# The bonus in a tile of its own, and the load of r, k, v on ACT's queue

## The chip, the cores and the metric

The kernel runs on one core of one Trainium2 chip. The metric is the device time of one execution in microseconds. The runs of the kernel before took 1875.28, 1884.89 and 1886.19 us, a median of 1884.89 us.

## The reference, cut to what matters

Two layers act on 1024 latent tokens and 256 context tokens of width 1024, all in fp32. The first layer mixes a short convolution with a gated recurrence of 8 heads of 64 (RWKV-7), run once forward and once in reverse. The second layer is latent attention. The change lies in the first layer, where the operands of the recurrence are prepared. For each direction the reference computes

```
decay, k_dir, b_vec = rwkv_direction(k, wl, al, kk, w0[d], w2[d], a0[d], a2[d], k_a)
y, state = rwkv7_scan(r, decay, k_dir, v, -kk, b_vec, state, reverse)
bonus[s] = bonus[s] + jnp.sum(r * k_dir * r_k, axis=-1, keepdims=True) * v
```

and later adds the bonus to the normalised output of the scan. The bonus of a token and a head is one number (the sum of r * k_dir * r_k over the 64 channels of the head, both directions together) times the vector v.

## The kernel before, in words

The input projections of layer 1 (`project`, L431 to L452) are matmuls in three split parts, 24 for each group of 512 tokens, written into two PSUM banks in turn (tag "p"). `shifted` (L536) makes r, k and v of a pair of heads j from them and stores them, with the normalised k, into `rkv_d[j]` in HBM, a tensor of 128 partitions by 4 parts by 1280 tokens (part 0 the normalised k, 1 r, 2 k, 3 v). Other projections (`zb`, `conv`) and the modulation of the layers (`ada`, L153) have no part in the recurrence's operands.

The operand stage (L849 to L883) runs over 20 units: 4 pairs of heads j times 5 groups q of 256 tokens. A unit has four parts. `decays(d)` (L633) makes the decay factors of direction d with two small products on PE, activations on ACT and a running sum on DVE (L647). `operands(d)` (L657) multiplies them with the parts of the unit's tile `x` on DVE: L667 and L668 write the tile AR, L669 and L670 the tile bk, L673 to L676 the tile BK, and in the second direction L680 and L681 write r * k_dir * r_k into x's part 2. `chunks(d)` (L683) forms products of 64-token chunks on PE (L690, L697), masks and copies them (L693 on DVE, L698 on ACT) and writes AR and M to HBM by nine DMAs (L701 to L709). `bonus` (L711) sums part 2 over the channels with a product on PE (L714), multiplies it with v into part 3 of the same tile x on DVE (L715), and writes that part to `bon_d` by two DMAs (L717).

`load_x` (L611) fetches the tile x of a unit, 512 KB, from `rkv_d`. x has two buffers. In the program's text the load for unit n+1 stands ahead of `operands(0)` of unit n (L867), so it takes the buffer that unit n-1 used, and may start when the last reader of that buffer is done.

Between the parts of a unit, `step` (L834) advances the chain of projections and the inversions (`invert`, L731) at the rates of L601. In this stage the order on PE is that of the text (`manual_schedule`, L507); on ACT, DVE, POOL and SP a planner puts the instructions in an order, and each engine and each of its DMA queues then runs its list in that order. ACT's queue issues the weights of the projections (L253) and of the modulation (L159), SP's nearly all other DMAs, POOL's those of the inversions of j below 3. ACT also empties the PSUM banks of the projections (L147 splits the next weights, L457, L467 and L543 read the products), and copies the modulation's product (L172), which PE transposes next (L176) and DVE adds up (L178). Squares of k are summed over the channels on PE at L575 and read on DVE at L576.

Of the kernel before, what the change touches and what calls it, by code (L numbers as in the profile page):

```python
# [9 lines left out]
F32 = mybir.dt.float32  # L10
# [3 lines left out]
ALU = mybir.AluOpType  # L14
# [4 lines left out]
P = 128  # L19
# [32 lines left out]
def build(ctx, tc, I, out, dbg=None):  # L52
    nc = tc.nc
    V, S, G, TE, SY = nc.vector, nc.scalar, nc.gpsimd, nc.tensor, nc.sync
# [12 lines left out]
    rkv_d = [dram.tile([P, 4, T], F32, name=f"rkv_d{j}") for j in range(4)]  # L67
    mix_d = [dram.tile([P, 4, T], F32, name=f"mix_d{i}") for i in range(2)]

    zb_d, bon_d = (dram.tile([P, 4, T], F32, name=n) for n in ("zb_d", "bon_d"))  # L70
# [200 lines left out]
    hs = (slice(0, 64), slice(64, 128))  # L271
# [41 lines left out]
    with ExitStack() as c2:  # L313
# [3 lines left out]
        xs = []  # L317
        for n0 in range(0, T, 256):
            x = x2.tile([P, KT, 256], F32, tag="x", name="x", bufs=5)
# [57 lines left out]
        for i in range(4):  # L377
            rest = []
            for n, x in enumerate(xs):
                s, cols = 1 if n == 0 else 0, slice(n * 256, n * 256 + 256)  # L380
                h, lo = H[:, 2 * i:2 * i + 2, cols], L[:, 2 * i:2 * i + 2, cols]
# [123 lines left out]
    with ExitStack() as c1:  # L505
# [4 lines left out]
        bp = cb.enter_context(tc.tile_pool(name="prep", bufs=1, side="right"))  # L510
        scanm = cc("scan")
        NB, N = 4, 256
# [96 lines left out]
        xs = []  # L609

        def load_x(j, q):  # L611
            xs.append(bp.tile([P, 4, N], F32, tag="x", name="x", bufs=2))
            SY.dma_start(out=xs[-1], in_=rkv_d[j][:, :, q * N:q * N + N])

        def load_w2(j):
            w = lp.tile([P, 2, P], F32, tag="w2", name="w2")
# [11 lines left out]
        def unit(j, q):  # L628

            n0, c0 = q * N, q * NB  # L630
# [80 lines left out]
            def bonus():  # L711
                x = xs.pop(0)
                ps = psb.tile([P, 512], F32, tag="b", name="b")
                TE.matmul(ps[:, :N], bones, x[:, 2], start=True, stop=True)  # L714
                V.tensor_tensor(x[:, 3], x[:, 3], ps[:, :N], op=ALU.mult)  # L715
                for h in range(2):
                    SY.dma_start(out=bon_d[hs[j % 2], j // 2 * 2 + h, n0:n0 + N], in_=x[hs[h], 3])  # L717

            return decays, operands, chunks, bonus

# [131 lines left out]
        split_w2()  # L852
        need(0)
        load_x(0, 0)
        us[0][0](0)
        us[0][0](1)
        for n, (j, q) in enumerate(uo):
            decays, operands, chunks, bonus = us[n]
            after = us[n + 1]
            if q == 4:  # L860
                need(j + 1)
            if q == 2 and j < 3:
                load_w2(j + 1)
            if q == 4 and j < 3:
                split_w2()
            if after:
                load_x(*uo[n + 1])  # L867
            operands(0)
            step(RATE[j][0])
            operands(1)  # L870
            if after:
                after[0](0)
            step(RATE[j][1])
            chunks(0)
            if after:
                after[0](1)
            step(RATE[j][2])
            chunks(1)
            bonus()
            step(RATE[j][3])  # L880
            if q == 4:
                advance(inv, 99)
                inv = invert(j)  # L883
# [71 lines left out]
    with ExitStack() as c1:  # L955
        c1.enter_context(tc.manual_schedule(engines={ET.PE, ET.DVE, ET.Activation}))
        op = c1.enter_context(tc.tile_pool(name="rw_scan0", bufs=1, side="right", reuse_waits="tile"))
# [155 lines left out]
    def products1(wh, wl, n0, n1, pool=ops, tag="o"):  # L1113
        ps = pool.tile([P, 512], F32, tag=tag, name="p")
        gemm3(ps[:, :n1 - n0], lambda kt: wh[:, kt, :], lambda kt: wl[:, kt, :],
              lambda kt: H[:, kt, n0:n1], lambda kt: L[:, kt, n0:n1], KT)
        return ps

    OUTM = {ET.PE}
    with ExitStack() as c1:  # L1120
# [44 lines left out]
        for x, q in enumerate(quarters):  # L1165
            n0, n1 = q * 256, q * 256 + 256
# [3 lines left out]
            xs = []  # L1170
            ps = [ops.tile([P, 512], F32, tag="o", name="o").rearrange("p (a b) -> p a b", a=2) for _ in range(4)]
# [60 lines left out]
    with ExitStack() as c1:  # L1232
# [106 lines left out]
        for x, (m, (n0, n1)) in enumerate(units):  # L1339
# [10 lines left out]
            if (m, n0) in early:  # L1350
                ps = early.pop((m, n0))
            else:
# [3 lines left out]
                ps = products1(*ready[m], n0, n1)  # L1356
# [12 lines left out]
    with ExitStack() as c1:  # L1369
# [196 lines left out]
        for x, (h, n) in enumerate(groups):  # L1566
# [4 lines left out]
            if (h, n) == (7, 0):  # L1571
                cw.close()
                clat.close()
                op = co.enter_context(tc.tile_pool(name="o_p", bufs=2, side="left"))
# [29 lines left out]
    with ExitStack() as c1:  # L1604
# [3 lines left out]
        for m, n0 in [(m + i, n) for m in range(0, 8, 2) for n in (0, 512) for i in range(2)]:  # L1608
# [5 lines left out]
            ps = ops.tile([P, 512], F32, tag="o", name="o")  # L1614
# [107 lines left out]
```

## Time and profile before

| | us |
|---|---|
| median of 3 runs | 1884.89 |
| profiled execution, its own time | 1887.55 |
| span of the profiled execution | 1885.8 |
| PE busy | 1719.4 (91%) |
| DVE busy | 1197.7 (64%) |
| ACT busy | 922.9 (49%) |
| POOL busy | 199.4 (11%) |

PE is TensorE (PEld its weight loads), DVE VectorE, ACT ScalarE, POOL GpSimd, SP SyncE. The operand stage lies between about 115 and 690 us of the span. Busy time is an average over stages; a gap on PE in one stage is read from PE's instructions there and from what ended the gap.

### The profile page before, as it was taken

The page shows a single profiled execution, that of the slowest core. Times are in us where ns is not written, and L with a number is a line of the kernel's source. Part 1 is how long each engine was busy: PE and PEld are TensorE (multiplying, and loading weights), DVE is VectorE, ACT ScalarE, POOL GpSimd, SP SyncE. Part 2 cuts the span into 40 slices and gives each one's busy share as a digit, 9 for nine tenths or more (in the row PEclk, how much of TensorE's full clock was granted, in tenths as well). Part 3 has the DMA queues.
Part 4 walks back from the last instruction along what each step waited for, and adds up shares of the span by engine and source line. Part 5 has one row for each costly group of instructions (what it writes and reads, how often), then busy time and mean ns, then how long its engine had stood idle before and what let it go on. Part 6 is the DMA issues. An engine that isn't in the chain of part 4 may idle for free.

```text
span 1885.8 us, 37021 instructions
## 1 busy us (share of the span) xinstructions
PE 1719.4 (91%) x14352; PEld 1480.7 (79%) x14352; DVE 1197.7 (64%) x2685; ACT 922.9 (49%) x2353; POOL 199.4 (11%) x230
## 2 busy tenths in 40 slices
PE   4999989889999979787899999999998999999999
PEld 3777867767778767776889978788888888888787
DVE  5747559738849745444378662558777777787822
ACT  4756444554444412555244342366666666666610
POOL 1200010220230300010043100000010010010000
PEclk9999999998999989898999999999999999999999
DMA  9067877997996854999644331210000010001242
GB/s 333 26 190 209 229 182 192 254 228 181 229 236 171 217 112 124 345 335 307 228 153 131 108 106 62 85 47 12 21 25 26 20 31 20 21 20 32 93 146 100
DMA packets 264575, 263.31 MB, mean 140 GB/s; under 512 B 63504, under 2 KB 226192, under 8 KB 263056
## 3 DMA queue, kind: packets, MB, share of 16 engines
q1 hardware_dynamic: 220528, 211.82, 38.5%
q10 hardware_dynamic: 37744, 33.03, 6.0%
q0 software_dynamic: 6128, 16.10, 3.7%
q8 instruction: 113, 1.85, 0.4%
q14 instruction: 62, 0.51, 0.1%
HBM read 164.90 MB, written 95.94 MB: 138 GB/s over the span
## 4 chain that ended last, share of the span: by engine, by line
PE 37%; DVE 12%; ACT 6%; DMA 6%; issue 4%; SPq 1%; POOL 0%; ACTq 0%; POOLq 0%; DVEq 0%
PE p L268 8%; PE s_ps L1486 5%; PE o L268 5%; PE p L444 3%; PE po L1525 3%; PE o L1179 3%; PE pk L268 3%; DVE mx L1489 2%; DVE pL L148 2%; PE pT L1513 2%; ACT jk L1436 1%; PE r_ps L1486 1%; DMA X<-v_d 1%; ACT p L1498 1%; PE y L1027 1%
## 5 line engine op out<-in xcount | busy, mean ns | idle before, releaser
L444 PE MATMUL p<-h0H,wh 128*128 128x512 f32 x744 | 277.4, 373 | 8.2 <-DVE th L458 7.3
L444 PE MATMUL p<-h0H,wl 128*128 128x512 f32 x744 | 267.4, 359 | 0.5 <-DVE wl L148 0.5
L444 PE MATMUL p<-h0L,wh 128*128 128x512 f32 x744 | 267.6, 360 | 0.0
L444 PEld LDWEIGHTS p<-h0H,wh 128*128 128x128 f32 x744 | 141.9, 191 | 32.7 <-DVE th L458 7.7
L444 PEld LDWEIGHTS p<-h0H,wl 128*128 128x128 f32 x744 | 141.4, 190 | 23.4 <-DVE wl L148 1.0
L444 PEld LDWEIGHTS p<-h0L,wh 128*128 128x128 f32 x744 | 141.7, 191 | 19.8
L147 ACT CAST pH<-pT 128x512 fp32r<-128x512 f32 x160 | 94.2, 589 | 75.6 <-PE pT L1513 72.9
L148 DVE TENSOR_TENSOR pL<-pT,pH 128x512 fp32r<-128x512 f32 x160 | 109.5, 685 | 30.6 <-ACT pH L147 29.3
L1486 PE MATMUL s_ps<-kH,q 128*128 128x512 f32 x256 | 108.1, 422 | 0.0
L1513 PE MATMUL pT<-cst,p 128*128 128x128 f32 x640 | 98.1, 275 | 10.1 <-DVE mx L1495 3.5
L1489 DVE TENSOR_REDUCE mx<-s_ps 128x1 f32<-128x512 f32 x128 | 87.5, 684 | 22.4 <-PE s_ps L1486 21.9
L1525 PE MATMUL po<-pL,vH 128*128 128x256 f32 x320 | 92.9, 290 | 6.0 <-DVE pL L148 5.2
L1525 PE MATMUL po<-pH,vH 128*128 128x256 f32 x320 | 95.8, 299 | 0.1
L1179 PE MATMUL o<-mh,woH 128*128 128x256 f32 x320 | 93.8, 293 | 0.8 <-DVE y L1074 0.5
L1513 PEld LDWEIGHTS pT<-cst,p 128*128 128x128 f32 x640 | 74.0, 140 | 23.2 <-DVE pL L148 6.3
L1179 PE MATMUL o<-ml,woH 128*128 128x256 f32 x320 | 91.7, 286 | 0.3 <-DVE ml L148 0.3
L1179 PE MATMUL o<-mh,woL 128*128 128x256 f32 x320 | 91.4, 286 | 0.0
L1525 PE MATMUL po<-pH,vL 128*128 128x256 f32 x320 | 90.2, 282 | 0.0
L1498 ACT ACTIVATE p<-s_ps,mx 128x512 f32<-128x512 f32 x128 | 87.6, 692 | 0.1
L1486 PE MATMUL s_ps<-kr,q 128*128 128x512 f32 x256 | 80.3, 395 | 0.2 <-DVE q L1471 0.2
L268 PE MATMUL p<-h1H,w1h 128*128 128x512 f32 x200 | 79.6, 398 | 0.7 <-ACT acc L1280 0.7
L268 PE MATMUL p<-h1H,w1l 128*128 128x512 f32 x200 | 78.0, 390 | 0.0
(346 smaller groups left out, 4606.8 us busy)
## 6 DMA issues: line engine op xcount, KB each, us to landing
G<-g_d SPq DMA_DIRECT2D x40, 512.0 KB, 6.3
G<-s_d SPq DMA_DIRECT2D x40, 512.0 KB, 6.8
adaw<-in_ada_w_dram ACTq DMA_DIRECT2D x32, 512.0 KB, 5.5
wr<-in_w_in_dram ACTq DMA_DIRECT2D x31, 512.0 KB, 4.6
x<-rkv_d SPq DMA_DIRECT2D x20, 512.0 KB, 5.8
g_d<-AR SPq DMA_DIRECT2D x80, 128.0 KB, 4.7
g_d<-M SPq DMA_DIRECT2D x80, 128.0 KB, 2.6
s_d<-M SPq DMA_DIRECT2D x80, 128.0 KB, 3.0
```

What stands on the lines that cost most here:

```text
L147: S.copy(H, x)
L148: eng.tensor_tensor(L, x, f(H), op=ALU.subtract)
L268: TE.matmul(ps, w(kt), x(kt), start=q == 0, stop=q == 3 * n - 1)
L444: TE.matmul(ps[:, :n1 - n0], w[:, kt, :], h[:, kt, n0:n1], start=kt + e == 0, stop=kt + e == KT + 1)
L1027: TE.matmul(out[c, j], block(j, h)[r], x(j, h)[r], start=first and j == 0, stop=last and j == 3, tile_position=(r.start, c.start))
L1179: TE.matmul(ps[m // 2][:, m % 2], w[m][:, 4 * e + kt, :], y[:, kt, :], start=e + m % 2 + kt + i == 0, stop=e + m % 2 + kt + i == 7)
L1436: S.activation(jk[:, :b - a], raw[:, i, a:b], AF.Square, accum_out=ss[:, i, e:e + 1])
L1486: TE.matmul(s, x, y[:, n0:n1], start=e == 0, stop=e == 4)
L1489: V.tensor_reduce(mxs[i][:, b:b + 1], s, axis=mybir.AxisListType.X, op=ALU.max)
L1498: S.activation(pt[:, n0:n1], s_ps[i][e - 1] if e else r_ps[:, i, :], AF.Exp, bias=mx[:, 4:5], accum_out=mx[:, 5 + e:6 + e])
L1513: TE.transpose(ps[:, e, i * P:(i + 1) * P], pts[h, n, i][:, (2 * k + e) * P:(2 * k + e + 1) * P], ident)
L1525: TE.matmul(o, a[:, 2 * k + e, :], b[:, e, :], start=k + e + q_ == 0, stop=k + e + q_ == 7)
```

## The change

`load_x` issues its DMA from ACT's queue in place of SP's. `bonus` writes its product into a new tile `bo` (128 partitions by 256 numbers, one buffer), and the two DMAs to `bon_d` read from there. So the readers of x after the change are instructions of DVE and PE alone (L667 to L670, L680, L681, L714, L715).

```
         def load_x(j, q):
             xs.append(bp.tile([P, 4, N], F32, tag="x", name="x", bufs=2))
-            SY.dma_start(out=xs[-1], in_=rkv_d[j][:, :, q * N:q * N + N])
+            S.dma_start(out=xs[-1], in_=rkv_d[j][:, :, q * N:q * N + N])
...
                 TE.matmul(ps[:, :N], bones, x[:, 2], start=True, stop=True)
-                V.tensor_tensor(x[:, 3], x[:, 3], ps[:, :N], op=ALU.mult)
+                bo = bp.tile([P, N], F32, tag="bo", name="bo")
+                V.tensor_tensor(bo, x[:, 3], ps[:, :N], op=ALU.mult)
                 for h in range(2):
-                    SY.dma_start(out=bon_d[hs[j % 2], j // 2 * 2 + h, n0:n0 + N], in_=x[hs[h], 3])
+                    SY.dma_start(out=bon_d[hs[j % 2], j // 2 * 2 + h, n0:n0 + N], in_=bo[hs[h]])
```

## Rows read from the trace of the kernel before

**Rows 1.** The page: span, and busy time of each engine.

```profile
span 1885.8 us, 37021 instructions
...
PE 1719.4 (91%) x14352; PEld 1480.7 (79%) x14352; DVE 1197.7 (64%) x2685; ACT 922.9 (49%) x2353; POOL 199.4 (11%) x230
```

**Rows 2.** Busy time by stretch: PE, PEld, DVE, ACT, POOL, then PEclk, DMA share, GB/s.

```profile
115.00:690.00 575.00, 526.96 (x4378) 436.07 (x4378) 376.63 (x773) 272.86 (x627) 75.82 (x108) 0.95 0.83 208
```

**Rows 3.** Timeline of PE: start, us, instruction, in brackets the idle time before it.

```profile
281.79 0.58 PE L176 MATMUL ada_pt<-cst,adae 128*128 128x2 f32 x2 [8.30 <-ACT adae L172]
...
365.41 1.97 PE L588 MATMUL m<-cst,ea 128*128 128x128 f32 x8 [5.78 <-ACT adae L172]
...
428.98 2.93 PE L575 MATMUL m<-sqk,cst 128*128 128x512 f32 x4 [11.12 <-DVE ada L178]
```

**Rows 4.** Timeline of ACT ahead of the first gap.

```profile
279.96 0.42 ACT L651 ACTIVATE E<-t 128x256 f32<-128x256 f32 x1 [9.40 <-DVE t L647]
...
281.48 0.26 ACT L172 COPY adae<-ada_ps 128x128 f32<-128x128 f32 x1
```

**Rows 5.** Timeline of DVE ahead of the gaps.

```profile
253.25 0.41 DVE L715 TENSOR_TENSOR x<-x,b 128x256 f32<-128x256 f32 x1
...
275.87 0.43 DVE L669 TENSOR_TENSOR bk<-bk,x 128x256 f32<-128x256 f32 x1 [9.08 <-DMA x<-rkv_d]
...
360.59 0.42 DVE L667 TENSOR_TENSOR AR<-x,E 128x256 f32<-128x256 f32 x1 [8.13 <-DMA g_d<-M]
...
396.97 0.41 DVE L715 TENSOR_TENSOR x<-x,b 128x256 f32<-128x256 f32 x1
...
423.92 0.43 DVE L669 TENSOR_TENSOR bk<-bk,x 128x256 f32<-128x256 f32 x1 [10.41 <-DMA x<-rkv_d]
...
428.77 0.15 DVE L178 TENSOR_TENSOR ada<-ada_pt,vec 128x2 f32<-128x2 f32 x1
```

**Rows 6.** Timeline of SP's queue, the bonus writes and the loads behind them.

```profile
260.39 1.53 SPq L717 DMA_DIRECT2D bon_d<-x  x2
...
271.11 0.56 SPq L613 DMA_DIRECT2D x<-rkv_d  x1
...
345.68 1.10 SPq L717 DMA_DIRECT2D bon_d<-x  x2
...
352.59 1.06 SPq L613 DMA_DIRECT2D x<-rkv_d  x1
...
404.80 1.88 SPq L717 DMA_DIRECT2D bon_d<-x  x2
...
411.80 0.56 SPq L613 DMA_DIRECT2D x<-rkv_d  x1
```

**Rows 7.** Waits of the stage: us in total, times, longest.

```profile
DVE bk L669 <- DMA x<-rkv_d: 41.2, 7, 10.4
...
SPq L613 <- DMA bon_d<-x: 27.5, 14, 7.2
...
SPq L717 <- DMA adaw<-in_ada_w_dram: 1.9, 1, 1.9
```

**Rows 8.** Timeline of ACT and its queue where a DMA issue held it.

```profile
411.05 0.55 ACTq L159 DMA_DIRECT2D adaw<-in_ada_w_dram  x1
411.64 0.84 ACT L644 ACTIVATE t<-b,dv 128x256 f32<-128x256 f32 x2 [2.76 <-DMA g_d<-AR]
...
468.90 0.34 ACTq L253 DMA_DIRECT2D wr<-in_w_in_dram  x1
469.28 1.08 ACT L589 COPY vt<-m 128x512 f32<-128x512 f32 x2 [4.18 <-DVE wl L148]
```

**Rows 9.** DMA issues: count, KB each, median us to landing.

```profile
wr<-in_w_in_dram ACTq DMA_DIRECT2D x31, 512.0 KB, 4.6
x<-rkv_d SPq DMA_DIRECT2D x20, 512.0 KB, 5.8
```

**Rows 10.** Busy time by stretch behind the gaps, columns as in rows 2.

```profile
280.00:290.00 10.00, 8.21 (x37) 6.99 (x38) 9.84 (x28) 3.63 (x9) 0.00 (x0) 0.58 0.98 269
...
360.00:370.00 10.00, 4.59 (x15) 4.00 (x16) 9.35 (x21) 4.93 (x13) 3.08 (x5) 0.67 0.90 262
...
430.00:440.00 10.00, 10.00 (x71) 8.00 (x70) 5.96 (x11) 6.75 (x8) 0.00 (x0) 0.75 0.62 130
```

## The prediction

> **What bounds the kernel now.** I read the page's busy times first: PE works for 91% of the span, so the time is PE's work plus PE's gaps [rows 1]. Then the busy time by stretch: in the operand stage, 115 to 690 us, PE is busy 526.96 of 575.00 us, so 48.0 us of gaps lie there, at a mean granted clock of 0.95; ACT and DVE have room (47% and 66%), the DMA engines little (share 0.83) [rows 2]. Then PE's timeline in that stage, for its longest gaps. The three before the last pair of heads are 8.30, 5.78 and 11.12 us, 25.2 us together and over half of the stage's idle time [rows 3]. In the order that PE must keep, each waits for a small modulation or norm step that has nothing to do with r, k and v.
>
> The reader should see why those steps are late. The first gap ends with ACT's copy at 281.48; ACT itself had stood 9.40 us at L651 behind DVE's running sum [rows 4], and DVE had stood 9.08 us at L669 for the tile x [rows 5]. The third ends with DVE's L178 at 428.77, and DVE had stood 10.41 us at L669, again for x, until 423.92 [rows 5]. Ahead of the second DVE stood 8.13 us at L667, the first reader of x in that unit; the row names a write of M as the last event, but the load of x had been issued at 352.59, 8.0 us before [rows 5, 6]. I count it to x, with the doubt kept for the range.
>
> Last, SP's queue: why is x late? The load of x is issued at 271.11, 352.59 and 411.80, that is 10.7, 6.9 and 7.0 us after the bonus writes that read the same buffer (260.39, 345.68, 404.80) [rows 6]. SP stood at L613 for the landing of the bonus 14 times, 27.5 us in all, and DVE then stood 7 times for x, 41.2 us in all [rows 7]. So DMA of the bonus, then load, then DVE is one chain, and PE pays where it is longest.
>
> **The change, part by part.** *The bonus in its own tile.* DVE's L715 keeps shape and length (0.41 us) [rows 5], so the arithmetic costs nothing more. The last reader of x becomes L715 in place of the bonus writes: the landing of a bonus leaves the chain. The new wait is that L715 must find `bo` free, that is, the bonus writes of the unit before landed. In these three places the next load, and so that landing, stood 6.9 to 10.7 us behind the issue [rows 6], and units are 575/20 = 28.8 us apart on average [rows 2]; I cost it at nothing. If SP fell a whole unit behind, DVE would stand at L715 and PE's L690 of the next unit would wait behind it.
>
> *How early x can now be issued.* The early bound is the end of L715: 253.66 for the load of 271.11 and 397.38 for that of 411.80, so 17.4 and 14.4 us earlier [rows 5, 6]. The late bound is no gain at all. Something between is likely, because a DMA issue here also waits for unrelated DMAs: SP's bonus write waited 1.9 us for a load of ACT's queue [rows 7], and an issue on ACT's queue at 411.05 kept ACT for 2.76 us until a write of AR from SP's queue had landed [rows 8]. SP's own bonus issues, at 260.39 and 404.80, came 6.7 and 7.4 us after L715 under the same restriction. I take the time of the bonus issue as the time of the new x issue, which is the middle of both bounds: 10.7, 6.9 and 7.0 us earlier. On ACT's queue, 512 KB land in 4.6 us at the median, on SP's in 5.8 [rows 9], so I leave the flight as it was.
>
> *What PE gets back.* DVE's waits shrink from 9.08, 8.13 and 10.41 to 0, 1.2 and 3.4 us. The first gap goes whole, 8.30. The second goes whole, 5.78, as its chain comes 6.9 us earlier. The third shrinks by 7.0 to 4.1 us. That is 21.1 us. After such a gap PE ran for a while at the lower of the clock's two levels (1.2 of 2.4 GHz): the slices behind the first two show a granted clock of 0.58 and 0.67 over 8.21 and 4.59 us of work, an estimated 3.4 and 1.5 us lost [rows 10]. These 4.9 us come back; behind the third gap, which stays, 10.00 x (1 - 0.75) = 2.5 us are lost as before. Gain: 26.0 us. Where the waits of the other units for x go (the rest of the 41.2 us), none of the three long gaps stands behind them [rows 3], so I count nothing.
>
> *The load on ACT's queue.* SP loses 20 issues of 0.56 us, 11.2 us in all [rows 6], and the waits of L613; what is queued behind on SP (AR and M, L701 to L709) is issued sooner. Nothing moves on POOL's queue. ACT gains 20 issues of about 0.55 us [rows 8], 11 us, beside its idle half: nothing on PE's path. But a waiting issue holds ACT's list, with the next decays and the PSUM reads (L457, L467, L543, L172) behind it, which PE needs. Bounds: nothing, where ACT is idle anyway, and 4.18 us a load, the length for which ACT stood at L589 behind its own weight load that waited for DVE's reading of that tile [rows 8]. No long PE gap came of either hold [rows 3], and two PSUM banks in turn cover one group of matmuls. I take 3 us over all loads, near the lower end, because the load follows L715 at a unit's end, where ACT has little left; the upper end is 18 x 4.18 = 75 us. The weights on ACT's queue (L159, L253) start one load later at worst, 5.8 us, and are fetched a projection ahead.
>
> *The planner.* It draws new orders for ACT, DVE and SP. The trace can't show them; I bound that by the largest PE gap of the stage, 11.12 us either way, and take nothing.
>
> *Sum.* 26.0 - 3 = 23.0 us off 1887.55 (span 1885.8 and 1.75 around it) is 1864.5; the profiled execution stands 2.66 above the median of the runs, so **1862 us**.
>
> **One rule against it.** The row says that x is late because its issue is gated, at 7 to 11 us a time [rows 6]. The Trainium skill, page "DMA: Bandwidth & Descriptors", section "Issuing engines are not separate DMA queues", says that DMAs issued from several engines run on the same 16 DMA engines and interleave, so that a second issuer saves the sequencer's issue time alone. By that the move between queues is worth nothing on PE's path and the whole gain must come from the tile `bo`.
>
> **The rivals.** *No gain (full DMA engines).* The stage's DMA share is 0.83 [rows 2]. An x that is issued 7 us earlier flies beside the chunk writes of the same unit, and both stretch; if the flight grows by what the issue gains, DVE's waits stay and the time is 1885, give or take 5. For it: the load of 411.80 was not read until 423.92, 12 us later, twice the median. Against it: the load of 271.11 was read after 4.8 us [rows 5, 6], though its issue was late. By the rule just cited this is what a mere change of queue would do.
>
> *The change doesn't do what it says.* If the planner puts the load so late in ACT's list that ACT reaches it only after 271 or 411, x is no earlier and the time is 1885 again. Against it: ACT stood idle for 9.40 us just then [rows 4].
>
> *Slower: ACT held at the load.* ACT reaches the load before L715 is done or before an older write of SP has landed, and stands with the PSUM reads behind it. If 18 loads each hand 4.18 us to PE, that is 75 - 26 = 49 us more than now, 1934; slower by 1% begins where a load hands over (26 + 19)/18 = 2.5 us; at the mean of both, 3.3 us, it gives 1919. For it: ACT empties both banks for PE. Against it: today's holds of 2.76 and 4.18 us left no such gap.
>
> *More than the sum.* All three gaps and their slow clocks go, 25.2 + 7.4 = 32.6 us, and the planner's new order takes a small one as well: 1848.
>
> **How the numbers follow.** What a measurement of this kernel can tell from no change is about 1%, 19 us. Chances: forecast 0.54, its own range 1850 to 1877; no gain 0.18; change without effect 0.07; ACT held 0.14; more than the sum 0.07. Faster than 1866 are the last and three quarters of the forecast: 0.47. Within 1%: the remaining 0.14 of the forecast, the two cases near 1885, and 0.01 of the held ACT: 0.40. Slower: 0.13. The range of 8 in 10 leaves out the held ACT and most of the case below 1850: 1848 to 1894, the upper end being no gain plus one new gap of 9 us.
>
> **What would show it.** Right: x's issue on ACT's queue within 8 us of L715's end; no wait of DVE for x over 4 us; the PE gaps that wait for L172 and L178 gone or under 5 us; the stage about 23 us shorter and everything behind it unchanged. Wrong: waits of ACT ended by DVE's L715 or by SP's writes with PE waiting for L172, L457 or L543 behind them (ACT held); x's flight at 10 us or more (full engines); or new PE gaps of the old size that wait for another engine (the planner's order).

## The result, and the profile after

The changed kernel took 1856.7 us, the median of 4 runs (1849.5 to 1860.54), against 1884.36 us for the kernel before in the same comparison: a ratio of 0.9861, 95% interval 0.9837 to 0.9886. It is faster by 1.4%. The forecast was 1862 us, with a range of 1848 to 1894. The profiled execution took 1854.03 us, 33.5 us less than that of before; the medians lie 27.7 us apart.

The page of the changed kernel, span and busy time of each engine:

```profile
span 1852.2 us, 37031 instructions
...
PE 1708.7 (92%) x14352; PEld 1471.5 (79%) x14352; DVE 1198.3 (65%) x2685; ACT 923.2 (50%) x2353; POOL 198.9 (11%) x230
```

Busy time by stretch in the changed kernel, columns as in rows 2. The same 575 us now hold 550.94 us of PE's work in place of 526.96, though the last 36.6 us of them belong to the next stage; the granted clock (the share of TensorE's full speed that it was given) is 0.99 in place of 0.95 [rows 2]:

```profile
115.00:690.00 575.00, 550.94 (x4545) 456.24 (x4544) 405.52 (x820) 277.88 (x635) 75.83 (x108) 0.99 0.81 210
```

Waits of PE in that stretch of the changed kernel (us in all, times, longest). Of the three gaps [rows 3], one is left, as 1.3 us (the row of L178):

```profile
PE p L444 <- DVE th L458: 5.5, 1, 5.5
PE m L786 <- DMA X<-bt_d: 4.4, 3, 2.7
PE m L786 <- DMA NQ<-g_d: 3.6, 2, 3.0
PE A L690 <- DVE M L693: 3.4, 5, 1.3
PE m L575 <- DVE sqk L576: 1.4, 1, 1.4
PE m L575 <- DVE ada L178: 1.3, 1, 1.3
```

Timeline of the changed kernel, DVE and ACT's queue, at the unit of the first gap. The new line L716 is the bonus product. The load of x goes out 0.03 us after its end, and DVE's L669 finds x there; in the kernel before it stood 9.08 us [rows 5], and the load came 17.4 us after the product [rows 5, 6]:

```profile
251.81 0.41 DVE L716 TENSOR_TENSOR bo<-x,b 128x256 f32<-128x256 f32 x1
...
252.25 0.53 ACTq L613 DMA_DIRECT2D x<-rkv_d  x1
...
266.08 0.40 DVE L669 TENSOR_TENSOR bk<-bk,x 128x256 f32<-128x256 f32 x1
```

PE's L176, which stood 8.30 us [rows 3], now follows its predecessor without a gap:

```profile
272.71 0.28 PE L176 MATMUL ada_pt<-cst,adae 128*128 128x2 f32 x2
```

DVE has no wait for x left at all (41.2 us in 7 waits before, [rows 7]), and the flight of x, from its issue to its landing, is shorter: 5.1 us at the median in place of 5.8 [rows 9]. The line L613 of the changed kernel:

```profile
L613 ACTq DMA_DIRECT2D x<-rkv_d x20: 525/533/556, 127.5 to 589.7; - x20
...
DMA to landing us min/median/max: 4.9/5.1/7.1
```

The stage is where the time went. The first projection after the last unit, PE's L444 behind DVE's L458, started at 684.94 us before and starts at 653.36 now: 31.6 of the 33.6 us of span were won ahead of it. This row is also the largest gap that is left there:

```profile
653.36 0.80 PE L444 MATMUL p<-h0H,wh 128*128 128x512 f32 x1 [5.47 <-DVE th L458]
```

Busy time up to that row, first before, then after. PE's idle time fell from 48.0 to 24.1 us, and its busy time from 521.9 to 514.3 us for the same work, at a granted clock of 0.99 in place of 0.96:

```profile
115.00:684.94 569.94, 521.90 (x4366) 432.06 (x4366) 371.91 (x761) 272.86 (x627) 75.82 (x108) 0.96 0.83 209
...
115.00:653.36 538.36, 514.30 (x4373) 425.52 (x4371) 371.72 (x761) 273.00 (x628) 75.83 (x108) 0.99 0.86 222
```

### The profile page after: what moved, and what is told of

It reads as the page before. It is cut to its first block, busy times and chain, and to the rows that moved or that the text cites. A ratio compares the mean times of both kernels' runs of the same rounds, so it can differ in the third digit from the quotient of the medians.

```text
span 1852.2 us, 37031 instructions
## 1 busy us (share of the span) xinstructions
PE 1708.7 (92%) x14352; PEld 1471.5 (79%) x14352; DVE 1198.3 (65%) x2685; ACT 923.2 (50%) x2353; POOL 198.9 (11%) x230
## 4 chain that ended last, share of the span: by engine, by line
PE 51%; DVE 20%; DMA 10%; ACT 9%; issue 6%; SPq 2%; POOL 1%; ACTq 0%; DVEq 0%; POOLq 0%
PE p L444 12%; PE p L268 8%; PE s_ps L1487 5%; PE o L268 5%; PE po L1526 3%; PE pk L268 3%; PE o L1180 2%; DVE mx L1490 2%; PE pT L1514 2%; DVE pL L148 2%; ACT jk L1437 1%; DVE BL L749 1%; PE y L1028 1%; DVE tm L747 1%; DMA adaw<-in_ada_w_dram 1%
## 5 line engine op out<-in xcount | busy, mean ns | idle before, releaser
L444 PE MATMUL p<-h0H,wh 128*128 128x512 f32 x744 | 276.6, 372 | 5.5 <-DVE th L458 5.5
L444 PE MATMUL p<-h0H,wl 128*128 128x512 f32 x744 | 267.0, 359 | 0.0
L444 PE MATMUL p<-h0L,wh 128*128 128x512 f32 x744 | 266.8, 359 | 0.0
L444 PEld LDWEIGHTS p<-h0H,wh 128*128 128x128 f32 x744 | 141.5, 190 | 29.2 <-DVE th L458 5.7
L444 PEld LDWEIGHTS p<-h0H,wl 128*128 128x128 f32 x744 | 141.1, 190 | 22.5 <-DVE wl L148 0.3
L444 PEld LDWEIGHTS p<-h0L,wh 128*128 128x128 f32 x744 | 141.5, 190 | 19.5
```

The costliest lines, as they stand in the source:

```text
L444: TE.matmul(ps[:, :n1 - n0], w[:, kt, :], h[:, kt, n0:n1], start=kt + e == 0, stop=kt + e == KT + 1)
```

## The experiments

Two theories were to be told apart: that x was late because the landing of the bonus writes released its buffer, and that SP's queue itself made it late. A third doubt was the planner's new order. The edits below are given against the changed kernel, unless they say otherwise.

**The tile alone** (the load back on SP's queue):

```
-            S.dma_start(out=xs[-1], in_=rkv_d[j][:, :, q * N:q * N + N])
+            SY.dma_start(out=xs[-1], in_=rkv_d[j][:, :, q * N:q * N + N])
```

> The bonus in its own tile, the load of x still on SP's queue. Theory (x was late because its buffer was released by the landing of the bonus writes): most of the gain is here; SP reaches the load after the writes ahead of it in its list, so x is issued some 4 to 8 us later than in the changed kernel, but no longer after the landing; no DVE wait for x over 4 us, PE gaps for L172 and L178 under 5 us, 1855 to 1868 us. Rival (SP's queue itself is what makes x late, whatever frees the buffer): x is issued 10 us or more after the bonus product as before, DVE waits over 30 us in all for x, and the time is 1878 to 1890 us.

Measured: 1866.34 us, ratio to the kernel before 0.9921 (0.9896 to 0.9947). With the kernel before at 1880.5 us on this chip, 14.2 us of gain. Its timeline of SP's queue shows the load behind the list of SP's writes; the bonus product of that unit had run from 282.12 to 282.53:

```profile
283.69 1.28 SPq L708 DMA_DIRECT2D s_d<-M  x2
285.01 0.61 SPq L709 DMA_DIRECT2D s_d<-M  x1
285.72 1.14 SPq L718 DMA_DIRECT2D bon_d<-bo  x2
286.96 0.57 SPq L613 DMA_DIRECT2D x<-rkv_d  x1
```

The load no longer waits for the landing: in this unit it is issued right behind the bonus issue, 4.4 us after the product. Over the 18 units that have a product before the load, that delay is 4.2 to 16.6 us, the longest where other writes of SP stand between. On average it is 6.7 us, against 10.2 us in the kernel before and 0.6 us in the changed one. The flight is 6.0 at the least, 6.5 at the median and 9.5 us at the most. What is left of DVE's waits for x, and PE's gaps that come of them, in that kernel:

```profile
DVE bk L669 <- DMA x<-rkv_d: 12.4, 6, 3.6
```

```profile
276.16 0.58 PE L176 MATMUL ada_pt<-cst,adae 128*128 128x2 f32 x2 [3.01 <-ACT adae L172]
...
413.85 2.93 PE L575 MATMUL m<-sqk,cst 128*128 128x512 f32 x4 [4.56 <-DVE ada L178]
```

Two of the three gaps are there again, at 3.01 and 4.56 us in place of 8.30 and 11.12 [rows 3]. The release theory's time and its bounds on the waits were met, and the rival's 1878 us and more was wrong. But the theory had most of the gain here, and 14.2 us is about half of it. What the changed kernel has besides is a load that doesn't stand in SP's list: it leaves 6.0 us earlier on average and flies 1.4 us less at the median.

**ACT's queue alone** (against the kernel before):

```
-            SY.dma_start(out=xs[-1], in_=rkv_d[j][:, :, q * N:q * N + N])
+            S.dma_start(out=xs[-1], in_=rkv_d[j][:, :, q * N:q * N + N])
```

> The load of x on ACT's queue, the bonus still written into x, so that the load waits for the landing of the bonus writes. Theory (release): nothing of the gain is here, and the wait now holds ACT instead of SP, 5 to 18 us at each of 18 loads with the PSUM reads behind it; PE gaps that end with ACT's L147, L457, L467, L543 or L172 appear; 1900 to 1960 us. Rival (the queue): x is issued as early as in the changed kernel, 1853 to 1868 us. A third way (ACT is idle enough): no change, 1878 to 1890 us.

Measured: 1887.78 us, ratio 1.004 (1.0024 to 1.0057): slightly slower, about 7 us. The theory's 1900 us and more was wrong, the queue rival's 1868 us and less too. The time lies in the range of the third way, but ACT wasn't idle enough, as its rows show. The loads went out 9.5 us after the product on average. The kernel's waits of DVE and ACT, and the issue that held ACT for one of them:

```profile
DVE bk L669 <- DMA x<-rkv_d: 24.1, 6, 9.2
...
ACT th L457 <- DMA bon_d<-x: 15.1, 1, 15.1
```

```profile
277.34 0.53 ACTq L613 DMA_DIRECT2D x<-rkv_d  x1
277.92 0.60 ACT L457 ACTIVATE th<-p 128x512 f32<-128x512 f32 x1 [15.07 <-DMA bon_d<-x]
```

ACT stood 15.07 us, held by the load at the head of its list, with the next decays behind it, and PE met both kinds of gap:

```profile
279.31 0.58 PE L641 MATMUL b<-wl,w2h 128*128 128x256 f32 x1 [6.08 <-ACT t L644]
...
432.19 2.93 PE L575 MATMUL m<-sqk,cst 128*128 128x512 f32 x4 [10.64 <-DVE ada L178]
```

**ACT held, with x early.** This separates a late x from a held ACT. After each load of x, from the second unit on, ACT's queue also reads 32 bytes of the bonus of the unit before into a scratch tile that nothing uses:

```
             if after:
                 load_x(*uo[n + 1])
+                if n:
+                    jp, qp = uo[n - 1]
+                    S.dma_start(out=scr[0:1, 0:8], in_=bon_d[hs[jp % 2], jp // 2 * 2 + 1, qp * N:qp * N + 8][0:1])
```

> The changed kernel, and after each load of x ACT's queue also issues a 32-byte read of the bonus of the unit before, which has to wait for that bonus to land; its data is used nowhere. So x is early as in the changed kernel, but ACT is held as in the kernel with the queue alone. Theory (two costs: a late x, and a held ACT): the hold by itself costs what the queue alone lost against the kernel before, 5 to 20 us: 1858 to 1876 us, with PE gaps ended by ACT's L147, L172, L543, L644 or L698. Rival (ACT has the time; the queue alone lost only because x was late): no PE gap ended by ACT over 2 us, 1848 to 1858 us.

Measured: 1869.53 us, ratio 0.992 (0.9894 to 0.9945). The time is the theory's, and DVE has no wait for x in the operand stage. The timeline of ACT shows x gone out in time, and the read that follows holding the list for 12.62 us:

```profile
259.56 0.53 ACTq L614 DMA_DIRECT2D x<-rkv_d  x1
...
275.24 0.25 ACTq L872 DMA_DIRECT2D scr<-bon_d  x1
275.53 0.60 ACT L457 ACTIVATE th<-p 128x512 f32<-128x512 f32 x1 [12.62 <-DMA g_d<-AR]
```

The releaser that this row names, a write of AR, is the event that came last by the profile; the read itself can only go out once the bonus has landed. Four other holds, 20.7 us together at ACT's L645, name the landing of the bonus. PE then stands where it stood in the kernel with the queue alone:

```profile
276.91 0.38 PE L642 MATMUL b<-wl,w2h 128*128 128x256 f32 x1 [3.65 <-ACT t L645]
...
354.85 0.38 PE L642 MATMUL b<-wl,w2h 128*128 128x256 f32 x1 [2.84 <-ACT t L645]
```

**The control: the same reads on POOL's queue** (`G.dma_start` in place of `S.dma_start` in the edit above).

> The same 32-byte reads issued from POOL's queue, as the control: the DMA is the same, but POOL is held in place of ACT. Theory: 1848 to 1860 us, as the changed kernel, since POOL's list is the inversions alone. Rival (the extra DMAs themselves, or a new order of the planner's, cost time): 1862 us or more.

Measured: 1852.53 us, ratio 0.9834 (0.981 to 0.9859), on the same chip. The reads cost nothing there, although POOL stood 332.0 us for them in all:

```profile
  DMA bon_d<-bo: 332.0, 18
```

So holding ACT costs 1869.53 - 1852.53 = 17.0 us, 0.94 us for each of 18 reads, and holding POOL costs nothing that was measured. That is more than the 7 us that the queue alone lost; there DVE's waits for x had shrunk too (24.1 us in place of 41.2), and the two effects weren't priced apart. Waits of PE in the kernel with ACT held show part of the 17.0 us; the first row is the gap at the stage's end, which was 5.3 us in the control:

```profile
PE p L444 <- DVE th L458: 9.2, 1, 9.2
PE b L642 <- ACT t L645: 7.2, 3, 3.7
```

The busy time up to the stage's L444 row, with ACT held and then in the control, shows the rest. PE is idle for 34.7 and 23.1 us, so 11.6 us went to waits; its work takes 520.1 and 513.8 us, so 6.3 us went to slower work, at a granted clock of 0.97 against 0.98:

```profile
115.00:669.80 554.80, 520.09 (x4376) 430.63 (x4374) 371.69 (x761) 273.10 (x628) 75.67 (x108) 0.97 0.83 215
...
115.00:651.88 536.88, 513.79 (x4363) 425.61 (x4361) 371.96 (x761) 272.31 (x627) 85.61 (x126) 0.98 0.85 222
```

**The load on POOL's queue** (`G.dma_start` in `load_x`).

> As the changed kernel, but the load of x on POOL's queue. Theory (release, and then a list that isn't held by other waits): POOL's list holds the inversions, at whose DMA issues and memsets it stood up to 172 and 78 us before; an x behind such a wait would come a unit or more late, PE gaps of 10 us and more, 1900 us or above for the units of j = 1 and later, unless the planner puts x ahead of them. Rival (any queue but SP's will do): 1850 to 1865 us, as the changed kernel.

Measured: 1850.69 us, ratio 0.9853 (0.9817 to 0.9889), as the changed kernel. The theory's 1900 us was wrong: the planner put the loads of x ahead of the inversions' long waits, and at 12 loads POOL stood ready before the product was done. In 16 of 18 units the load went out 0.3 us after it. Waits of POOL in that kernel:

```profile
POOL x L613 <- DVE bo L716: 199.4, 12, 27.7
```

In these runs what mattered of the queue was that nothing late stood ahead of the load in its list, and that nothing PE needed stood behind a load that still had to wait.

**Two buffers for the bonus tile** (`bufs=2` for `bo`).

> As the changed kernel, with two buffers for the bonus tile in place of one. The change of buffers takes no wait away if the tile was always free in time. Theory (release): same as the changed kernel, 1850 to 1861 us, and DVE's L716 never waits for a bonus write in either. Rival (the gain is a lucky order of the planner's): any small edit may draw another order, and the time strays by 10 us or more from 1857.

Measured: 1850.6 us, ratio 0.9847 (0.981 to 0.9885). No different from the changed kernel, whose medians were 1856.7 us and, run again, 1851.0 us. One buffer is enough: no wait of DVE for a bonus write is in the trace of the changed kernel. The planner drew DVE the same order in the operand stage as in the changed kernel, so this run says little of the rival, a lucky order. POOL's and the control do: there DVE's order is another one, and the time is 1850.7 and 1852.5 us, so the gain isn't one lucky order.

**The gap that is left at the stage's end.** Two steps of the projections ahead of the last inversion's first step:

```
         for n, _ in enumerate(inv):
+            if n == 0:
+                advance(chain, 2)
             owed += TAIL[n > 30]
```

> The changed kernel, with the projections advanced by two steps between the loads of the last inversion and its first step, so that DVE has L458 done before it stands at the inversion for its blocks. Theory (the 5.47 us gap of PE at 653 us, ended by DVE's L458, is on the path): that gap goes, with the slow clock behind it, 4 to 8 us: 1848 to 1853 us. Rival (the inversion's own chain sets the end of this stretch, and the projections are only moved): no change, 1854 to 1860 us.

Measured: 1848.45 us, ratio 0.9823 (0.9799 to 0.9848): in the theory's range, and the gap is gone. With four steps in place of two:

> The same with four steps in place of two. Theory: the gap goes as with two, but the inversion's first step can be late behind the projections' DVE work; 1848 to 1855 us. Rival: less filling is left for the end of the inversion, where PE then waits; 1856 to 1864 us.

Measured: 1856.2 us, ratio 0.9857 (0.9842 to 0.9872): the gain is gone, 7.8 us against two steps on the same chip. PE has new waits at 707 to 711 us for blocks of the inversion (L786, 3.66 and 1.30 us for X), as the rival had it, and the time is in the rival's range and above the theory's 1855. The two-step version was then run again beside the changed kernel, and beside a third with x on POOL's queue as well:

> The changed kernel with the projections advanced by two steps ahead of the last inversion's first step, with x on ACT's queue, in more rounds. Theory (PE's 5.47 us gap is on the path): 1846 to 1851 us, 4 to 8 us under the changed kernel on the same chip. Rival: within 2 us of it.

> The changed kernel once more, on the same chip as the two beside it, as their measure. Every theory: 1850 to 1860 us.

> The changed kernel with the load of x on POOL's queue and the projections advanced by two steps ahead of the last inversion's first step. Theory (both edits are on PE's path or beside it, and add): 1844 to 1850 us, faster than the changed kernel by 5 us or more. Rival (POOL and ACT are worth the same, and the tail's gap was not on the path): 1851 to 1858 us, no different from the changed kernel.

Measured on one chip: the changed kernel 1851.0 us (1848.48 to 1858.41), with two steps 1846.5 us (1844.59 to 1847.41), with POOL's queue besides 1849.14 us (1848.91 to 1849.33); the kernel before 1879.9 us. The ratio of the two-step version to the kernel before is 0.9816 (0.9794 to 0.9839). Its runs and those of the changed kernel don't overlap, so it is ahead of both kernels, by some 4.5 us over the changed one; with 4 and 6 runs, and 10 us between the runs of the changed kernel, that figure is rough. Its stretch behind the last unit, and the same stretch in the changed kernel, which was busy 34.33 of 40 us there at a clock of 0.91:

```profile
640.00:680.00 40.00, 40.00 (x208) 33.94 (x207) 30.85 (x54) 7.02 (x10) 1.40 (x2) 1.00 0.32 70
```

In the 50 us behind it, to 730 us, PE is busy 43.00 us at a clock of 0.83, against 45.56 at 0.90 in the changed kernel, so part of this is only moved.

POOL's queue adds nothing to ACT's. With it the time lies in the expected range, but 1.9 us under the changed kernel, not the 5 us expected, and 2.6 us above ACT's queue with the same two steps.

## Why the prediction was right

**What bounds the kernel** was read rightly. With x early the three PE gaps are 0, 0 and 1.3 us. The doubt on the second, where DVE's row named a write of M [rows 5], is settled in part. It vanished with the tile alone too. In the kernel with ACT's queue alone x was late in that unit, and DVE's row names it:

```profile
364.48 0.43 DVE L669 TENSOR_TENSOR bk<-bk,x 128x256 f32<-128x256 f32 x1 [7.60 <-DMA x<-rkv_d]
```

PE, which came to that L588 later there (369.80 in place of 365.41), found it ready. So DVE's wait was x's; that all of PE's 5.78 us came of it is likely, and not shown apart.

**The chain from the bonus's landing** was half of the matter. The tile alone took 14.2 us, ACT's queue alone lost 7, and both together took 27.7 (28.9 in the later comparison). The parts don't add. The tile lets the load go before the landing; the queue lets it go before SP's other writes. The mean delay of the load behind the product tells the same: 10.2 us before, 6.7 with the tile alone, 9.5 with the queue alone, 0.6 with both. On ACT without the tile, the load waits for the landing still, and holds ACT.

**How early x is issued** was mis-sized, on the safe side. I put it at the issue of the bonus write, 6.9 to 10.7 us earlier, for fear that ACT's issue would wait for unrelated DMAs. It goes out within 0.05 us of the product in 13 of 18 units and within 3.4 us in the others. (Nor was my figure quite the middle of my bounds, which is 8.7 and 7.2 us.) It fits the tile alone: there the load comes 6.7 us after the product on average, and I had the bonus issue at 6.7 and 7.4 us.

That kernel also shows what my forecast would have been worth had x gone out when I said. I priced it at 26.0 us; with the tile alone the stage's L444 row comes at 665.49 us, 19.5 us earlier than before, and the medians lie 14.2 us apart. The first gap kept 3.01 us where I had none, and PE's busy time to that row fell by 0.8 us where I had 4.9 back. So x came earlier than I thought, and the earliness that I assumed was worth less than I thought. The two errors work against each other, and that the forecast lies within 5.3 us of the measured time is in part luck.

**What PE gets back** in the changed kernel follows from the earlier x: 25.2 - 1.3 = 23.9 us of gaps in place of 21.1, and the slow clock behind all three, estimated at 3.4 + 1.5 + 2.5 = 7.4 us from rows 10, in place of 4.9. Together 31.3 us, of the 31.6 us by which the stage ended earlier. The busy times to the L444 row bear both out: PE's idle time fell by 24.0 us and its work by 7.6. What lies behind that row took 1200.9 us before and 1198.8 after.

**The load on ACT's queue**: I took 3 us off for a held ACT. In the changed kernel the loads left within 3.4 us of the product, and in the stage no wait of PE over 0.4 us was put down to ACT, so that term is near nothing. The longest hold at a load of x was, by its row, for an unrelated write of M, as I had feared of ACT's issues, and PE had no gap of it:

```profile
385.14 0.53 ACTq L613 DMA_DIRECT2D x<-rkv_d  x1
385.77 1.05 ACT L147 CAST wh<-wr 128x1024 fp32r<-128x1024 f32 x1 [3.34 <-DMA s_d<-M]
```

The price of a real hold, 0.94 us a read, lies well under my upper bound of 4.18 and under the 2.5 us from which the change would have been slower by 1%.

**The rivals.** *Full DMA engines*: refuted; the flight of x fell from 5.8 to 5.1 us at the median and from 11.5 to 7.1 at the most, at a DMA share of 0.86 up to the stage's L444 row (0.83 before). Of the rule of the Trainium skill, page "DMA: Bandwidth & Descriptors", section "Issuing engines are not separate DMA queues": by it the whole gain would come from the tile, and the trace differs, since the tile alone gives 14.2 us and the queue the rest. That doesn't speak against shared DMA engines; what the second issuer saved here was the place in SP's list, 4.4 us at the load shown and 6.0 us on average, and 1.4 us of flight at the median. *No effect*: refuted, in 13 of 18 units the load was first in ACT's list when the product was done. *ACT held*: the mechanism is real, and shown by the held kernel; the change doesn't meet it because the tile took the late release away. *More than the sum*: this is what the profiled execution did (33.5 us against the 32.6 of that case); the medians lie between it and the forecast.

## What to carry to other kernels

Where a load waits for its buffer, look at who reads the buffer last: if that is a write to HBM, a small tile for the write takes the write's flight, and with another queue its queueing too, out of the load's way. Here a load came 3.5 us earlier on average with the tile alone, and 9.5 us with the queue changed as well. Then give the load a queue in whose list nothing late stands ahead of it, and none whose engine PE depends on unless the load's last wait is over by the time the list gets there. The two edits belong together; alone, one gave half of the gain, and the other lost a little.

## What the runs showed that was not expected

With the extra reads ACT stood up to 12.6 us behind one waiting DMA issue, with PSUM reads behind it, and the kernel lost only 0.94 us a read on average. POOL stood 199 us in all at 12 of its loads and 332 us at the control's reads, and the kernel lost nothing. Four projection steps at the stage's end in place of two cost 7.8 us on the same chip, and so gave back all that two had won.
